# Eight products of low weights ahead of eight of high weights, in four chunks of a float32 encoder's up projections

## The chip, the cores and the metric

The kernel runs on one core of one Trainium2 chip. The metric is the device time of one execution in microseconds (us); the time of a kernel is the median of its runs. The profile is of one further execution.

## What is computed

The reference is a two-layer encoder on 256 tokens of width 2048, in float32. Each layer has a token mixer and then a gated channel mixer, each with a norm before and after and a residual add:

```python
def conv_glu(h, w_up, conv_w, conv_b, w_down):
    u = h @ w_up
    gate, val = u[..., :D_FF], u[..., D_FF:]
    gate = depthwise_conv3(gate, conv_w, conv_b)
    return (jax.nn.gelu(gate, approximate=False) * val) @ w_down
...
    for i in range(DEPTH):
        p = layers[i]
        h = rms_norm(x, p['mix_pre'])
        if i % 2 == 0:
            m = mixer_dilated_gqa(h, *p['mixer'], pos, row, col)
        else:
            m = mixer_mla(h, *p['mixer'], pos)
        x = x + rms_norm(m, p['mix_post'])
        h = rms_norm(x, p['ffn_pre'])
        x = x + rms_norm(conv_glu(h, *p['ffn']), p['ffn_post'])
```

The change concerns `h @ w_up` alone, with D_FF = 5632: half of its columns make the gate, half the value.

## The kernel before

**High and low halves.** TensorE multiplies in a rounded 32-bit format (F32R). To keep float32 accuracy, each operand is parted in two: a high half, which is the rounded number, and a low half, which is what the rounding left. A product of two numbers is then high x high + high x low + low x high.

**Weights.** All weights come as chunks of 128 x 1024 float32 (512 KB), in one fixed list. SyncE loads a chunk into one of four `raw` buffers (line 103). ScalarE casts it to the high half `whi` (line 117), and VectorE subtracts that from `raw` and writes the low half `wlo` (line 118). Both halves have three buffers each. `weights()` is called once per chunk: it sees that the chunks up to two ahead of the one it returns are split, and that the next ones are loading. The cast of the chunk three ahead has to wait until TensorE has read the high buffer that it will overwrite, and the subtraction in the same way for the low buffer.

**The up projection.** `ffn` loops over 11 groups of 512 gate columns and 512 value columns. For each group it calls `proj_t` twice: the gate projection (accumulators tagged `acc`) and then the value projection (tagged `at`). Here the weights are the stationary operand and the normed input is the moving one. The input tile of a block k has 512 columns: its high half for the 256 tokens, then its low half. So one product of high weights (line 186, 512 columns wide) gives high x high and high x low side by side in one accumulator, and one product of low weights (line 187, 256 wide) adds low x high to the first 256 columns; the two column halves are added later by `joined`. A `proj_t` has 8 chunks of weights, numbered 0 to 7, and four accumulators; a chunk holds two blocks k for each of the four accumulators, so it makes 8 high and 8 low products, high and low in turn. Each product brings its own load of 128 x 128 weights.

**What else runs.** While a value projection goes on, ScalarE and VectorE finish the gate of the same group (lines 247 to 248 and 911 to 917) and split the coming chunks. Between them the instructions of an engine stand in the order in which a scheduler put them; waits between engines are semaphores.

**Other products that the prediction speaks of.** `mm3` (lines 172 to 174) makes the three products of a block one after another. In `proj_pair` (layer 1) all of them are 256 wide, with weights as the stationary operand; in `proj_tok`, as the output projection of layer 0 uses it, all are 512 wide.

Of the kernel before, what the change touches and what calls it, by code (L numbers as in the profile page):

```python
# [16 lines left out]
P = 128  # L17
T = 256
D = 2048
KD = D // P  # L20
# [17 lines left out]
class Model:  # L38
# [134 lines left out]
        mm(ps, lh, rl, start=False, stop=False)  # L173
        mm(ps, ll, rh, start=False, stop=stop)  # L174

    def proj_t(self, nk, x, tag):

        mm = self.nc.tensor.matmul
        out = [self.psum(tag) for _ in range(4)]
        for c in range(nk // 2):  # L180
            hi, lo = self.weights()
            for i in range(4):
                for kk in range(2):
                    k = 2 * c + kk
                    s = slice(kk * 512 + i * P, kk * 512 + (i + 1) * P)
                    mm(out[i], hi[:, s], x(k), start=k == 0, stop=False)  # L186
                    mm(out[i][:, :T], lo[:, s], x(k)[:, :T], start=False, stop=k == nk - 1)  # L187
            self.tick()
        return out

# [703 lines left out]
    def ffn(self, layer, pre):  # L894
        nc, tc = self.nc, self.tc
        with tc.tile_pool(name=f"ffn{layer}", bufs=1) as sp:
            xs = self.xhl
            x = lambda k: xs[k // 4][:, k % 4].rearrange("p a t -> p (a t)")
            gh = [sp.tile([P, 4, T], F32R, name=f"gh{i}") for i in range(NFG)]
            gl = [sp.tile([P, 4, T], F32R, name=f"gl{i}") for i in range(NFG)]  # L900
            cw = lambda j, c: self.gain(f"l{layer}_conv_w", j * KF + c)
            norm = self.now(self.pre_norm(sp))
            for gi in range(NFG):
                pg = self.proj_t(KD, x, "acc")
                self.finish(norm)
                act = []
                for i in range(4):
                    c = 4 * gi + i
                    g = self.joined(sp, sp.tile([P, T], F32, tag="g", name="g", bufs=2), pg[i])
                    y = sp.tile([P, T], F32, tag="yf", name="yf", bufs=4)  # L910
                    nc.vector.tensor_tensor(out=g, in0=g, in1=self.rb, op=ALU.mult)
                    nc.scalar.activation(y, g, AF.Identity, scale=cw(1, c), bias=self.gain(f"l{layer}_conv_b", c))
                    nc.vector.scalar_tensor_tensor(out=y[:, 1:], in0=g[:, :T - 1], scalar=cw(0, c), in1=y[:, 1:],
                                                   op0=ALU.mult, op1=ALU.add)
                    nc.vector.scalar_tensor_tensor(out=y[:, :T - 1], in0=g[:, 1:], scalar=cw(2, c),
                                                   in1=y[:, :T - 1], op0=ALU.mult, op1=ALU.add)
                    nc.scalar.activation(y, y, AF.Gelu)
                    act.append(y)
                pv = self.proj_t(KD, x, "at")
                for i in range(4):  # L920
                    u = self.joined(sp, sp.tile([P, T], F32, tag="u", name="u", bufs=2), pv[i])
                    nc.vector.tensor_tensor(out=u, in0=u, in1=self.rb, op=ALU.mult)
                    nc.vector.tensor_tensor(out=u, in0=u, in1=act[i], op=ALU.mult)
                    self.parted(gh[gi][:, i, :], gl[gi][:, i, :], u)
            g = lambda k: (gh[k // 4][:, k % 4, :], gl[k // 4][:, k % 4, :])
            return self.out_proj(KF, g, 2 * layer + 1, pre, (sp, "m3", 1))
# [22 lines left out]
    def all_chunks(self):  # L949
        a = self.a  # L950
        groups = lambda w, gs: [w[g, c] for g in gs for c in range(w.shape[1])]
        out = groups(a["w_in0"], [8, 6, 7, 0, 2, 4, 1, 3, 5])
        out += [a["w_out0"][g, c] for g in range(4) for c in (4, 5, 6, 7, 0, 1, 2, 3)]
        ffn = lambda l: groups(a[f"w_up{l}"], [g for j in range(NFG) for g in (j, NFG + j)]) + \
            groups(a[f"w_down{l}"], range(4))
        out += ffn(0)
        out += groups(a["w_in1"], [0, 1]) + [a["w_kr"]]
        for p in range(8):
            out += groups(a["w_qr"], [p // 4]) if p % 4 == 0 else []
            out += [a["w_qn"][p], a["w_kn"][p]]  # L960
            out += groups(a["w_v"], [p // 2]) if p % 2 == 0 else []
        out += groups(a["w_out1"], range(4))
        out += ffn(1)
        return out
# [67 lines left out]
```

## Time and profile before

| | us |
|---|---|
| median of 3 runs | 2072.75 |
| lowest and highest of them | 2072.56, 2081.7 |
| the profiled execution | 2072.57 |
| its span, first to last instruction | 2070.8 |
| TensorE busy in the span | 2057.9 |
| VectorE busy | 1340.6 |
| ScalarE busy | 1084.6 |

Engines in the profile are PE (TensorE's products), PEld (its weight loads), DVE (VectorE), ACT (ScalarE), POOL and SP. A row of a group gives the line, engine, operation, the tiles written and read, shape and count; then the busy time in us and the mean of one in ns; then the idle time ahead of them and what ended it. A row of a timeline gives the start in us from the start of the span, the duration in us, engine, line, operation and count; a bracket gives the idle time before it and what released it. The granted clock of TensorE was 0.999 of full speed.

### The profile page before, as it was taken

How to read it: one execution, taken by the hardware profiler on the slowest of the kernel's cores; microseconds unless marked ns; L12 is line 12 of the kernel's file. 1: busy time of each engine (PE TensorE's matmuls, PEld its weight loads, DVE VectorE, ACT ScalarE, POOL GpSimd, SP SyncE). 2: the span in 40 equal slices, each digit the busy share in tenths (PEclk: the TensorE clock that was granted, in tenths of full speed). 3: DMA queues.
4: the chain of work that ended last, by engine and by line, in shares of the span. 5: the costliest groups of instructions: out<-in, count | busy, mean ns of one | idle time of the engine just before them, and what ended most of it. 6: DMA issues, size and time to landing. Idle time of an engine off the chain costs nothing.

```text
span 2070.8 us, 28951 instructions
## 1 busy us (share of the span) xinstructions
PE 2057.9 (99%) x10977; PEld 1764.1 (85%) x10977; DVE 1340.6 (65%) x2051; ACT 1084.6 (52%) x1695; POOL 0.2 (0%) x4
## 2 busy tenths in 40 slices
PE   9999999999999999999999999999999999999998
PEld 7888888888888888888888998888888888888886
DVE  6877757667667667444466875666766766754444
ACT  6655546555555555344455654555555555544443
POOL 0000000000000000000000000000000000000000
PEclk9999999999999999999999999999999999999999
DMA  8545565666666666666665445566666666666664
GB/s 315 176 153 163 164 200 174 186 193 190 188 192 191 187 192 190 196 198 199 198 186 170 125 129 177 177 188 190 185 195 191 188 191 190 185 200 198 198 194 154
DMA packets 108716, 385.96 MB, mean 186 GB/s; under 512 B 12064, under 2 KB 12576, under 8 KB 108576
## 3 DMA queue, kind: packets, MB, share of 16 engines
q1 hardware_dynamic: 108288, 383.83, 60.6%
q8 instruction: 86, 1.41, 0.3%
q14 instruction: 54, 0.44, 0.1%
q10 hardware_dynamic: 288, 0.28, 0.0%
HBM read 381.96 MB, written 2.10 MB: 185 GB/s over the span
## 4 chain that ended last, share of the span: by engine, by line
PE 98%; DVE 1%; ACT 0%; DMA 0%; issue 0%; DVEq 0%; SPq 0%
PE ps L186 31%; PE ps L172 16%; PE ps L174 16%; PE ps L173 16%; PE ps L187 16%; PE ps L463 1%; PE ps L242 1%; DVE x L383 1%; PE ps L405 0%; DMA raw<-in_w_in 0%; PE ps L790 0%; DVE wlo L118 0%; ACT junk L282 0%; PE ps L238 0%; DVE xhl L517 0%
## 5 line engine op out<-in xcount | busy, mean ns | idle before, releaser
L118 DVE TENSOR_TENSOR wlo<-raw,whi 128x1024 fp32r<-128x1024 f32 (+1 forms) x710 | 867.9, 1223 | 672.1 <-ACT whi L117 670.4
L117 ACT CAST whi<-raw 128x1024 fp32r<-128x1024 f32 (+1 forms) x710 | 745.9, 1052 | 786.5 <-PE ps L174 417.5
L186 PE MATMUL ps<-xhl,whi 128*128 128x512 f32 x2816 | 978.6, 394 | 1.0 <-DVE xhl L517 1.0
L187 PE MATMUL ps<-xhl,wlo 128*128 128x256 f32 x2816 | 779.2, 277 | 0.0
L186 PEld LDWEIGHTS ps<-xhl,whi 128*128 128x128 f32 x2816 | 527.6, 188 | 123.2 <-DVE xhl L517 1.9
L187 PEld LDWEIGHTS ps<-xhl,wlo 128*128 128x128 f32 x2816 | 528.7, 188 | 1.1 <-DVE wlo L118 0.5
L172 PE MATMUL ps<-whi,gh 128*128 128x512 f32 x704 | 273.9, 389 | 0.0
L174 PE MATMUL ps<-whi,gl 128*128 128x512 f32 x704 | 273.9, 389 | 0.0
L173 PE MATMUL ps<-wlo,gh 128*128 128x512 f32 x704 | 273.9, 389 | 0.0
L174 PEld LDWEIGHTS ps<-whi,gl 128*128 128x128 f32 x704 | 132.2, 188 | 27.7
L173 PEld LDWEIGHTS ps<-wlo,gh 128*128 128x128 f32 x704 | 132.2, 188 | 27.4
L172 PEld LDWEIGHTS ps<-whi,gh 128*128 128x128 f32 x704 | 132.2, 188 | 27.1
L172 PE MATMUL ps<-whi,xhl 128*128 128x512 f32 x352 | 138.8, 396 | 1.3 <-ACT whi L117 1.2
L173 PE MATMUL ps<-wlo,xhl 128*128 128x512 f32 x352 | 137.6, 391 | 0.0
L174 PE MATMUL ps<-whi,xhl 128*128 128x512 f32 x352 | 137.1, 391 | 0.0
L172 PE MATMUL ps<-whi,oh 128*128 128x512 f32 x256 | 100.0, 390 | 0.0
L173 PE MATMUL ps<-wlo,oh 128*128 128x512 f32 x256 | 99.7, 389 | 0.0
L174 PE MATMUL ps<-whi,ol 128*128 128x512 f32 x256 | 99.6, 389 | 0.0
L247 ACT COPY half<-ps 128x256 f32<-128x256 f32 x176 | 65.0, 369 | 45.6 <-PE ps L186 36.0
L172 PEld LDWEIGHTS ps<-whi,xhl 128*128 128x128 f32 x352 | 66.0, 188 | 15.1 <-ACT whi L117 1.5
L174 PEld LDWEIGHTS ps<-whi,xhl 128*128 128x128 f32 x352 | 66.0, 188 | 13.9
L173 PEld LDWEIGHTS ps<-wlo,xhl 128*128 128x128 f32 x352 | 66.3, 188 | 13.4 <-DVE wlo L118 0.9
(186 smaller groups left out, 1584.9 us busy)
## 6 DMA issues: line engine op xcount, KB each, us to landing
raw<-in_w_up SPq DMA_DIRECT2D x352, 512.0 KB, 4.1
raw<-in_w_down SPq DMA_DIRECT2D x176, 512.0 KB, 4.2
raw<-in_w_in SPq DMA_DIRECT2D x88, 512.0 KB, 3.8
raw<-in_w_out SPq DMA_DIRECT2D x64, 512.0 KB, 3.9
gb<-in_post SPq DMA_DIRECT2D x16, 256.0 KB, 3.9
raw<-in_w_qn SPq DMA_DIRECT2D x8, 512.0 KB, 3.6
raw<-in_w_kn SPq DMA_DIRECT2D x8, 512.0 KB, 3.6
raw<-in_w_v SPq DMA_DIRECT2D x8, 512.0 KB, 3.6
```

The lines of the kernel that those rows point to most:

```text
L117: self.nc.scalar.copy(hi[:, s], raw[:, s])
L118: self.nc.vector.tensor_tensor(out=lo[:, s], in0=raw[:, s], in1=hi[:, s].bitcast(F32), op=ALU.subtract)
L172: mm(ps, lh, rh, start=start, stop=False)
L173: mm(ps, lh, rl, start=False, stop=False)
L174: mm(ps, ll, rh, start=False, stop=stop)
L186: mm(out[i], hi[:, s], x(k), start=k == 0, stop=False)
L187: mm(out[i][:, :T], lo[:, s], x(k)[:, :T], start=False, stop=k == nk - 1)
L242: self.tc.keep_in_program_order(self.nc.tensor.transpose(out, x, self.ident))
L247: self.nc.scalar.copy(b, ps[:, T:])
L383: return nc.vector.scalar_tensor_tensor(out=x, in0=m[c][:, t, s], scalar=r[t], in1=x, op0=ALU.mult, op1=ALU.add)
L463: nc.tensor.matmul(ps[:, i, :], l, r, start=n == 0, stop=n == len(pairs) - 1))
```

## The change

In `proj_t` a new argument `apart` names one chunk in which all eight low products come first and then all eight high ones, each in the same order of accumulators and blocks as before. In all other chunks high and low alternate as they did. `ffn` passes 4, the fifth of eight chunks, for the value projection of the first two groups, so four chunks of the program are concerned: two in each layer.

```diff
-    def proj_t(self, nk, x, tag):
+    def proj_t(self, nk, x, tag, apart=None):
...
             hi, lo = self.weights()
-            for i in range(4):
-                for kk in range(2):
-                    k = 2 * c + kk
-                    s = slice(kk * 512 + i * P, kk * 512 + (i + 1) * P)
-                    mm(out[i], hi[:, s], x(k), start=k == 0, stop=False)
-                    mm(out[i][:, :T], lo[:, s], x(k)[:, :T], start=False, stop=k == nk - 1)
+            blocks = [(i, 2 * c + kk, slice(kk * 512 + i * P, kk * 512 + (i + 1) * P))
+                      for i in range(4) for kk in range(2)]
+            high = lambda i, k, s: mm(out[i], hi[:, s], x(k), start=k == 0, stop=False)
+            low = lambda i, k, s: mm(out[i][:, :T], lo[:, s], x(k)[:, :T], start=False, stop=k == nk - 1)
+            for products in ((low,), (high,)) if c == apart else ((high, low),):
+                for b in blocks:
+                    for product in products:
+                        product(*b)
             self.tick()
...
-                pv = self.proj_t(KD, x, "at")
+                pv = self.proj_t(KD, x, "at", 4 if gi < 2 else None)
```

On TensorE, at the fifth chunk of layer 0's first value projection, this stands before. The four `ps` are the accumulators, `xhl2` the input, `whi_3507` and `wlo_3508` the halves of this chunk's weights; `wlo_3486` belongs to the chunk before.

```order
L187 MATMUL ps_3458<-xhl1_3171,wlo_3486 128x256
L186 MATMUL ps_3455<-xhl2_3244,whi_3507 128x512
L187 MATMUL ps_3455<-xhl2_3244,wlo_3508 128x256
L186 MATMUL ps_3455<-xhl2_3244,whi_3507 128x512
L187 MATMUL ps_3455<-xhl2_3244,wlo_3508 128x256
L186 MATMUL ps_3456<-xhl2_3244,whi_3507 128x512
L187 MATMUL ps_3456<-xhl2_3244,wlo_3508 128x256
L186 MATMUL ps_3456<-xhl2_3244,whi_3507 128x512
L187 MATMUL ps_3456<-xhl2_3244,wlo_3508 128x256
```

The other two accumulators go on in the same way. In the changed kernel the same place reads as follows (lines 187 and 188 are there what 186 and 187 are before, and `whi_3529` belongs to the next chunk):

```order
L188 MATMUL ps_3458<-xhl1_3171,wlo_3486 128x256
L188 MATMUL ps_3455<-xhl2_3244,wlo_3508 128x256 x2
L188 MATMUL ps_3456<-xhl2_3244,wlo_3508 128x256 x2
L188 MATMUL ps_3457<-xhl2_3244,wlo_3508 128x256 x2
L188 MATMUL ps_3458<-xhl2_3244,wlo_3508 128x256 x2
L187 MATMUL ps_3455<-xhl2_3244,whi_3507 128x512 x2
L187 MATMUL ps_3456<-xhl2_3244,whi_3507 128x512 x2
L187 MATMUL ps_3457<-xhl2_3244,whi_3507 128x512 x2
L187 MATMUL ps_3458<-xhl2_3244,whi_3507 128x512 x2
L187 MATMUL ps_3455<-xhl2_3244,whi_3529 128x512
```

The eight low products have moved ahead of the eight high ones; the three other chunks read alike, and nothing else on TensorE has moved. The instructions of VectorE, ScalarE and SyncE stand in the same order as before. Only a wait differs: on VectorE, the subtractions around chunk 7's (`wlo_3574`) with the engines and queues that each waits for, before:

```order
L118 TENSOR_TENSOR wlo_3508<-raw_3392,whi_3507 128x1024 [waits DMAHW4_49,PE_49,Activation_49]
L118 TENSOR_TENSOR wlo_3530<-raw_3467,whi_3529 128x1024 [waits DMAHW5_49,PE_49,Activation_49]
L118 TENSOR_TENSOR wlo_3552<-raw_3489,whi_3551 128x1024 [waits DMAHW6_49,PE_49,Activation_49]
L118 TENSOR_TENSOR wlo_3574<-raw_3511,whi_3573 128x1024 [waits DMAHW7_49,PE_49,Activation_49]
L118 TENSOR_TENSOR wlo_3596<-raw_3533,whi_3595 128x1024 [waits DMAHW0_49,PE_49,Activation_49]
```

and in the changed kernel:

```order
L118 TENSOR_TENSOR wlo_3508<-raw_3392,whi_3507 128x1024 [waits DMAHW4_49,PE_49,Activation_49]
L118 TENSOR_TENSOR wlo_3530<-raw_3467,whi_3529 128x1024 [waits DMAHW5_49,PE_49,Activation_49]
L118 TENSOR_TENSOR wlo_3552<-raw_3489,whi_3551 128x1024 [waits DMAHW6_49,PE_49,Activation_49]
L118 TENSOR_TENSOR wlo_3574<-raw_3511,whi_3573 128x1024 [waits DMAHW7_49,Activation_49]
L118 TENSOR_TENSOR wlo_3596<-raw_3533,whi_3595 128x1024 [waits DMAHW0_49,PE_49,Activation_49]
```

The subtraction of chunk 7 reuses the low buffer of chunk 4, and no longer waits for TensorE itself: the cast that it waits for has waited for a later product of that chunk.

## The prediction

> **What bounds the kernel now.** I read the page first, for what fills the span and for the chain that ended last; then the list of waits of TensorE's weight loads, since what the change turns round is the order in which TensorE asks for its two kinds of weights; then the timeline of TensorE, VectorE and ScalarE around the four chunks that change. The page's rows:
>
> ```profile
> span 2070.8 us, 28951 instructions
> PE 2057.9 (99%) x10977; PEld 1764.1 (85%) x10977; DVE 1340.6 (65%) x2051; ACT 1084.6 (52%) x1695; POOL 0.2 (0%) x4
> PE 98%; DVE 1%; ACT 0%; DMA 0%; issue 0%; DVEq 0%; SPq 0%
> L186 PE MATMUL ps<-xhl,whi 128*128 128x512 f32 x2816 | 978.6, 394 | 1.0 <-DVE xhl L517 1.0
> L187 PE MATMUL ps<-xhl,wlo 128*128 128x256 f32 x2816 | 779.2, 277 | 0.0
> L187 PEld LDWEIGHTS ps<-xhl,wlo 128*128 128x128 f32 x2816 | 528.7, 188 | 1.1 <-DVE wlo L118 0.5
> ```
>
> TensorE is busy for 99% of the span and makes up 98% of the chain that ended last. Nothing else sets the end, so the change is worth what it does to TensorE's stream of products, plus any idle time that it puts into that stream. The two lines that it reorders, 186 (a product of high weights, 512 columns wide) and 187 (of low weights, 256 wide), are the products of the up projections; they had practically no idle time ahead of them. Next, who kept the weight loads of line 187 waiting, over the whole program:
>
> ```profile
> engine line waited for: us in total, times, longest us
> PEld ps L187 <- DVE wlo L118: 0.5, 2, 0.3
> ```
>
> Twice in 2816 loads a low product found its low weights not yet written, and 0.5 us was lost. That is the dependence that the change draws forward, and the profile says that it almost never binds. Then one of the four changed chunks, the fifth of layer 0's first value projection, on TensorE's timeline (start, duration, engine, line):
>
> ```profile
> 368.23 0.39 PE L186 MATMUL ps<-xhl,whi 128*128 128x512 f32 x1
> 368.46 0.27 PE L187 MATMUL ps<-xhl,wlo 128*128 128x256 f32 x1
> 368.57 0.40 PE L186 MATMUL ps<-xhl,whi 128*128 128x512 f32 x1
> ...
> 370.65 0.40 PE L186 MATMUL ps<-xhl,whi 128*128 128x512 f32 x1
> 370.88 0.28 PE L187 MATMUL ps<-xhl,wlo 128*128 128x256 f32 x1
> 371.00 0.39 PE L186 MATMUL ps<-xhl,whi 128*128 128x512 f32 x1
> ```
>
> What to see here is the spacing of starts, not the durations. A low product follows its high one after 0.23 us, the next high one after 0.11, and the chunk of sixteen takes 371.00 - 368.23 = 2.77 us. The printed durations add up to 8 x (0.394 + 0.277) = 5.4 us, twice that; the page says that matmuls are pipelined and that their ends are modelled. So I cost the change by distances between starts. The four changed chunks together are 4 x 2.77 = 11.1 us of the 2070.8.
>
> **Part 1, the same products in another order.** Nothing is added or removed: eight high and eight low products before, and eight of each after. What changes is which product follows which. A chunk was eight times high-low and low-high; it becomes seven times low-low, once low-high, seven times high-high and once high to the next chunk's high. The trace has long runs of both new neighbours elsewhere. The pair projection of layer 1 issues 24 products of 256 columns one after another, and the output projection of layer 0 issues 33 of 512 columns; of each run the first and the last row:
>
> ```profile
> 1128.89 0.28 PE L172 MATMUL ps<-ckv,whi 128*128 128x256 f32 x1
> 1131.63 0.28 PE L174 MATMUL ps<-ckv,wlo 128*128 128x256 f32 x1
> 319.78 0.39 PE L172 MATMUL ps<-whi,oh 128*128 128x512 f32 x1
> 327.04 0.40 PE L174 MATMUL ps<-whi,ol 128*128 128x512 f32 x1
> ```
>
> The narrow run has 23 steps in 2.74 us, 0.119 us a step; the wide run has 32 steps in 7.26 us, 0.227 a step. Every product in them brings its own weight load, as here, and consecutive ones add into the same accumulator, as here. A changed chunk is then 8 x 0.119 + 8 x 0.227 = 0.953 + 1.815 = 2.77 us, against 2.77 now. The difference is under the 0.01 us in which the timeline is printed: a narrow product costs 0.01 more behind a narrow one than a wide product costs behind it, and a wide one saves as much by not standing ahead of a narrow one. I take 0.00 us a chunk.
>
> The bounds come from further rows. The best that the narrow products could do is the 0.11 us seen in the chunk above between a low start and the next; 8 x 0.11 + 1.815 = 2.70, a gain of 0.07 a chunk and 0.3 us over four. The worst is that a run of low products is paced by its weight loads, each with the 0.188 us of the page's row: 8 x (0.188 - 0.119) = 0.55 us a chunk, 2.2 us in all. Were it paced by the whole modelled product of 0.277, that would be 8 x (0.277 - 0.119) = 1.26 a chunk, 5.1 us in all. The nearest row by far is the narrow run, with the same shape, the same kind of weights and the same accumulation, and it decides.
>
> The Trainium skill, page "TensorE: Matmul & The Clock Gate", section "LDWEIGHTS (loading the stationary operand)", gives a weight load as its columns divided by 1.2 in ns: an estimate of 107 ns for 128 columns, not the recorded 188. By the page a load just fits under a narrow product and the sum stays 0.00; by the recorded load it would be +2.2 us. The narrow run's 0.119 us a step agrees with the page.
>
> The Trainium skill, page "Perfetto Trace Analysis", section "Tensor Engine Instruction (MATMUL, LD_WEIGHTS)", adds that the end of a matmul is computed from its size, not observed. By that the 277 ns is no price and the 5.1 us falls away; the 2.77 us chunk against 5.4 us of durations bears it out.
>
> **Part 2, the low weights are wanted first.** The first product of the chunk waited for the cast of the high half (ScalarE, line 117) and the second, 0.23 us later, for the subtraction that makes the low half (VectorE, line 118). Now the first one waits for VectorE. Behind that wait stand all the later products in TensorE's queue, so a late subtraction would cost its full lateness. The four subtractions that belong to the four chunks, and the starts of the three other chunks:
>
> ```profile
> 365.30 1.22 DVE L118 TENSOR_TENSOR wlo<-raw,whi 128x1024 fp32r<-128x1024 f32 x1
> 409.68 1.22 DVE L118 TENSOR_TENSOR wlo<-raw,whi 128x1024 fp32r<-128x1024 f32 x1
> 1365.48 1.22 DVE L118 TENSOR_TENSOR wlo<-raw,whi 128x1024 fp32r<-128x1024 f32 x1
> 1409.86 1.23 DVE L118 TENSOR_TENSOR wlo<-raw,whi 128x1024 fp32r<-128x1024 f32 x1
> 412.60 0.39 PE L186 MATMUL ps<-xhl,whi 128*128 128x512 f32 x1
> 1368.41 0.39 PE L186 MATMUL ps<-xhl,whi 128*128 128x512 f32 x1
> 1412.79 0.39 PE L186 MATMUL ps<-xhl,whi 128*128 128x512 f32 x1
> ```
>
> The low halves are ready at 366.52, 410.90, 1366.70 and 1411.09, and the chunks start at 368.23, 412.60, 1368.41 and 1412.79. That is 1.71, 1.70, 1.71 and 1.70 us of cover, after the 0.23 us by which the demand moves forward has been taken off. What hides the edit is that weights are split two chunks ahead of their use; if that cover were gone, the cost would be what the subtraction is late by. Cost 0.
>
> **Part 3, the buffers come free at other times.** Each half has three buffers, so the cast for chunk 7 waits for the last high product of chunk 4. On ScalarE's timeline that cast, then the subtraction behind it on VectorE's, then the start of chunk 7 on TensorE's:
>
> ```profile
> 371.08 1.05 ACT L117 CAST whi<-raw 128x1024 fp32r<-128x1024 f32 x1 [1.72 <-PE ps L186]
> 372.17 1.23 DVE L118 TENSOR_TENSOR wlo<-raw,whi 128x1024 fp32r<-128x1024 f32 x1 [1.55 <-ACT whi L117]
> 376.55 0.39 PE L186 MATMUL ps<-xhl,whi 128*128 128x512 f32 x1
> ```
>
> The last high product starts at 370.65 now, and becomes the last product of the chunk: 371.00 - 0.23 = 370.77. So the cast starts 0.12 us later, at about 371.20, and its subtraction ends at about 373.52 instead of 373.40. Chunk 7 starts at 376.55, so 3.0 us of cover are left. The next cast waits for chunk 5 and doesn't feel it. The low half of chunk 4 comes free about 1.8 us earlier (its last reader starts near 369.07, not 370.88), and the subtraction of chunk 7 loses its wait for TensorE; but it was released by the cast (the row says so), so it gains nothing. The queues of the loads, of ScalarE and of the output are not reordered. Cost 0.
>
> The sum is 0.00 + 0 + 0, four times. The profiled execution took 2072.57 us, of which 2070.8 are its span and 1.8 lie around it; the median of the three runs is 2072.75, 0.2 above. I forecast 2072.6 us.
>
> **The rivals.** *A run of narrow products is paced by its weight loads* (slower). Place: the first half of each changed chunk. It decides as soon as one load in a row of them takes TensorE longer than the 0.119 us step. Price 2.2 us with the recorded 0.188, giving 2074.8, and 5.1 with the modelled 0.277, giving 2077.7. For it speaks the recorded load, longer than the step; against it stand 23 steps at 0.119, each with such a load. I give it 0.05.
>
> *The early demand for the low half is met late* (slower). It decides once VectorE ends the subtraction over 1.7 us later than in the rows above; a whole further subtraction put in ahead (1.22) would not do it. Two of them ahead would be 0.7 us late, 3 us over four chunks, giving 2075.6. VectorE's order is unchanged, so I give it 0.02.
>
> *The alternation itself costs something* (faster). If the narrow products in a row took 0.11, the gain is 0.3 us, giving 2072.3; earlier free low buffers could add at most the 0.5 us of waits on line 187, giving 2071.8. I give it 0.05, mostly for the first half of it. That the change does nothing at all is excluded for the order on TensorE, which does change in these four places.
>
> **How the numbers follow.** My forecast of no change gets 0.83, the three rivals 0.12, and 0.05 is left for something that these rows don't show. A measurement of this kernel can tell about 0.5% from no change, 10.4 us, and that is nearly as long as the four changed chunks together: to be slower by so much they would have to take almost twice their time, and to be faster by so much they would have to vanish. Every case above therefore lies within 0.5%. The 0.05 is divided as 0.02 faster and 0.03 slower, the larger part on the slow side because one of the three runs shown lies at 2081.7, 9 us above the other two. So faster 0.02, same 0.95, slower 0.03. The range runs from 2070.5, which is the lowest case less about 1 us for another run, to 2077.7, the dearest bound.
>
> **What would show it right or wrong.** In the profile of the changed kernel each of the four chunks should show eight low starts about 0.12 apart, then eight high ones about 0.23 apart, 2.77 us from the first to the next chunk's first. Part 1 is wrong if the low starts stand 0.15 or more apart, or if high products behind high ones stand nearer than 0.22. Part 2 is wrong if the weight loads of the low products wait for line 118 more often than twice. Part 3 is wrong if chunk 7's cast moves by more than 0.2 us, or if a product of chunk 7 waits. The forecast as a whole is wrong if the span moves by more than 5 us, and then its cause would have to lie outside these chunks.

## The result, and the profile after

| | us |
|---|---|
| changed kernel, median of 5 runs | 2089.95 (2089.70 to 2090.27) |
| kernel before, median of 5 runs, the three shown above among them | 2072.65 (2072.56 to 2081.70) |
| ratio | 1.0075, 95% interval 1.0054 to 1.0095 |
| span of the profiled execution | 2087.9, before 2070.8 |

The change costs 17.3 us, 0.75%. The range ended at 2077.7: the forecast of no change was wrong. The page of the changed kernel:

```profile
span 2087.9 us, 28951 instructions
PE 2076.0 (99%) x10977; PEld 1772.8 (85%) x10977; DVE 1340.3 (64%) x2051; ACT 1081.4 (52%) x1695; POOL 0.2 (0%) x4
PE 98%; DVE 1%; ACT 0%; DMA 0%; issue 0%; DVEq 0%; SPq 0%
L187 PE MATMUL ps<-xhl,whi 128*128 128x512 f32 x2816 | 992.3, 399 | 1.0 <-DVE xhl L522 1.0
L188 PE MATMUL ps<-xhl,wlo 128*128 128x256 f32 x2816 | 784.1, 281 | 0.0
```

TensorE waits no more than it did. It is busy for 99% again, with the same number of products, and its busy time has grown by 18 us. Only the two lines of the up projection became dearer (lines 187 and 188 are 186 and 187 of before); the large groups of `mm3`, 389 to 396 ns each before, are where they were. So the time lies in products that run at a lower pace, not in a gap. Where they lie shows in the answer for the line of the high products, asked for each layer apart: behind the count stand the shortest, median and longest duration in ns, then the starts of the first and of the last product in us. In the kernel before:

```profile
L186 PE MATMUL ps<-xhl,whi x1408: 387/395/501, 331.3 to 822.7; 128*128 128x512 f32 x176
L186 PE MATMUL ps<-xhl,whi x1408: 390/395/504, 1331.6 to 1822.9; 128*128 128x512 f32 x176
```

In the changed kernel:

```profile
L187 PE MATMUL ps<-xhl,whi x1408: 387/398/500, 331.1 to 831.1; 128*128 128x512 f32 x176
L187 PE MATMUL ps<-xhl,whi x1408: 389/398/505, 1340.0 to 1840.0; 128*128 128x512 f32 x176
```

The up projection took 491.4 and 491.3 us and takes 500.0 and 500.0 now: 8.6 + 8.7 = 17.3 us, the whole result. Next the changed chunk itself on TensorE's timeline. Neighbours of one line are merged, so the nine low products begin with the last one of chunk 3, and the nine high ones end with the first one of chunk 5:

```profile
367.88 1.23 PE L188 MATMUL ps<-xhl,wlo 128*128 128x256 f32 x9
368.94 2.23 PE L187 MATMUL ps<-xhl,whi 128*128 128x512 f32 x9
371.01 0.28 PE L188 MATMUL ps<-xhl,wlo 128*128 128x256 f32 x1
```

From the last low product of chunk 3 to the first high one stand nine steps in 1.06 us, 0.118 each; from there to the next low one nine in 2.07, 0.230 each. That is close to the 0.119 and 0.227 of the prediction, and a chunk that costs nearly what it did. But 130 us later, in chunks whose order was not touched, the stream looks otherwise than in the kernel before, which shows this:

```profile
499.96 0.39 PE L186 MATMUL ps<-xhl,whi 128*128 128x512 f32 x1
500.19 0.27 PE L187 MATMUL ps<-xhl,wlo 128*128 128x256 f32 x1
500.31 0.40 PE L186 MATMUL ps<-xhl,whi 128*128 128x512 f32 x1
500.54 0.28 PE L187 MATMUL ps<-xhl,wlo 128*128 128x256 f32 x1
500.65 0.39 PE L186 MATMUL ps<-xhl,whi 128*128 128x512 f32 x1
```

The changed kernel at the same time:

```profile
500.05 0.40 PE L187 MATMUL ps<-xhl,whi 128*128 128x512 f32 x1
500.28 0.28 PE L188 MATMUL ps<-xhl,wlo 128*128 128x256 f32 x1
500.40 0.40 PE L187 MATMUL ps<-xhl,whi 128*128 128x512 f32 x1
500.64 0.28 PE L188 MATMUL ps<-xhl,wlo 128*128 128x256 f32 x1
500.76 0.40 PE L187 MATMUL ps<-xhl,whi 128*128 128x512 f32 x1
501.00 0.28 PE L188 MATMUL ps<-xhl,wlo 128*128 128x256 f32 x1
501.11 0.40 PE L187 MATMUL ps<-xhl,whi 128*128 128x512 f32 x1
```

Before, the pattern repeats every two pairs (0.39, 0.27, 0.40, 0.28) in 0.69 us. After, it repeats every three pairs in 1.06 us, with steps of 0.24 between a high and a low product, which the other pattern doesn't have. From the third group to the last chunk, 143 chunks, a chunk takes 2.773 us in the one and 2.827 us in the other. In a layer 162 chunks of the old order follow the first changed one: 162 x 0.0533 = 8.6 us. I call the two a rhythm of two pairs and a rhythm of three pairs.

**Theory:** the alternating stream has more than one stable rhythm; the changed chunk breaks the running one, the stream falls into the three-pair rhythm, and it stays there until the projection ends. **Rivals:** each changed chunk costs 17.3 / 4 = 4.3 us of its own; or ScalarE, VectorE and the loads have come into another phase to TensorE and disturb it; or the new program as such is slower (where its code or buffers lie).

### The profile page after: what moved, and what is told of

It is laid out like the page before. It is cut to its first block, busy times and chain, and to the rows that moved or that the text cites. A ratio compares the mean times of both kernels' runs of the same rounds, so it can differ in the third digit from the quotient of the medians.

```text
span 2087.9 us, 28951 instructions
## 1 busy us (share of the span) xinstructions
PE 2076.0 (99%) x10977; PEld 1772.8 (85%) x10977; DVE 1340.3 (64%) x2051; ACT 1081.4 (52%) x1695; POOL 0.2 (0%) x4
## 4 chain that ended last, share of the span: by engine, by line
PE 98%; DVE 1%; ACT 0%; DMA 0%; issue 0%; DVEq 0%; SPq 0%
PE ps L187 32%; PE ps L188 16%; PE ps L172 16%; PE ps L173 16%; PE ps L174 16%; PE ps L468 1%; PE ps L247 1%; DVE x L388 1%; PE ps L410 0%; DMA raw<-in_w_in 0%; PE ps L795 0%; DVE wlo L118 0%; ACT junk L287 0%; PE ps L243 0%; DVE xhl L522 0%
## 5 line engine op out<-in xcount | busy, mean ns | idle before, releaser
L187 PE MATMUL ps<-xhl,whi 128*128 128x512 f32 x2816 | 992.3, 399 | 1.0 <-DVE xhl L522 1.0
```

The costliest lines, as they stand in the source:

```text
L187: high = lambda i, k, s: mm(out[i], hi[:, s], x(k), start=k == 0, stop=False)
```

## The experiments

All edits are against the changed kernel; the last experiment has none. Over the experiments the runs of the kernel before fell into three groups, near 2072.6, 2081.5 and, three times, 2090.5; what these are is shown by the last experiment, and medians are to be compared with 2072.6.

**Changed chunks only in the last group.**

```diff
-                pv = self.proj_t(KD, x, "at", 4 if gi < 2 else None)
+                pv = self.proj_t(KD, x, "at", 4 if gi == NFG - 1 else None)
```

> The changed chunk is moved from the first two groups to the eleventh, last one, of each layer: two changed chunks in all. Rhythm theory (the alternating stream of products has two steady rhythms, 0.347 and 0.353 us a pair; a changed chunk throws it into the slow one, which lasts to the end of the layer's up projection): only 3 chunks of 8 pairs follow in each layer, 2 x 24 x 0.0063 = 0.3 us, so 2073.0. If each changed chunk instead costs 17.3 / 4 = 4.3 us wherever it stands: 2081.3. If the mere presence of such chunks slows the whole program (placement of code or buffers): about 2090.

Measured: median 2073.15 us, ratio 1.0012 (0.9989 to 1.0035). The same reordering, placed at the end of the stream, is nearly free: the six shorter runs lie between 2072.62 and 2073.34. So a changed chunk has no price of 4.3 us of its own. Of the other four runs three lay near 2081.6 and one at 2090.5, as runs of the kernel before do.

**Changed chunks only in the first group.**

```diff
+                pv = self.proj_t(KD, x, "at", 4 if gi == 0 else None)
```

> The changed chunk is kept in the first group of each layer and dropped in the second: two changed chunks. Rhythm theory: the first one has thrown the stream into the slow rhythm and nothing brings it back, 163 chunks of 8 pairs in each of two layers at 0.0063 us more, 16.4 us and the transients, so 2089 to 2090, as with four. A price for each changed chunk: 2072.7 + 8.6 = 2081.3.

Measured: 2089.98 us, ratio 1.0069 (1.0043 to 1.0096). Two changed chunks cost as much as four. The price lies in what follows.

**A break behind the changed chunks.**

```diff
+                if gi == 2:
+                    self.warm(1)
                 pg = self.proj_t(KD, x, "acc")
```

> The changed kernel with one small product of zeros (bfloat16, 256 wide) issued ahead of the third group of each layer: a break in the stream after both changed chunks. Rhythm theory: the break is an occasion to fall into either rhythm. If it falls into the fast one, the slow stretch is from chunk 4 of the first value projection to the end of the second group, 20 chunks in each layer: 2 x 20 x 0.05 = 2 us, so 2075; if into the slow one, 2090. If side engines or the placement of code slow the stream, one small product changes nothing: 2090. So 2075 would speak for a rhythm alone; 2090 would leave it open.

Measured: 2074.81 us, all ten runs between 2074.49 and 2075.10, ratio 0.9992 (0.9976 to 1.0009). The line of the high products, by layer:

```profile
L187 PE MATMUL ps<-xhl,whi x1408: 387/395/505, 331.2 to 823.6; 128*128 128x512 f32 x176
L187 PE MATMUL ps<-xhl,whi x1408: 389/395/504, 1332.6 to 1825.0; 128*128 128x512 f32 x176
```

492.4 us in each layer instead of 500.0: one product of zeros in each layer, ahead of the third group, takes 15.1 of the 17.3 us back. The changed chunks are all still there. The rival of the new program as such falls with this run, and that of a price for each changed chunk once more.

**Without the side traffic.** In groups 4 to 8 every chunk uses one and the same pair of weight halves, and the list of weights to load leaves those groups out, so the kernel computes something else.

```diff
+            if keep is None or c == 0 and not self.kept:
+                self.kept = self.weights()
+            hi, lo = self.kept
...
+                keep = True if 4 <= gi < 9 else None
```

> The changed kernel, but in groups 4 to 8 of each layer (counted from 0) every chunk uses one and the same pair of weight halves: no weights are loaded, cast or subtracted there, and 80 chunks of each layer have only the gate and value work on ScalarE and VectorE beside the products. The output is therefore another. Rhythm theory: the slow rhythm is TensorE's own, and these chunks still take 2.83 us. Contention theory (from the changed chunk on, ScalarE, VectorE or the loads stand in another phase to TensorE and take its memory accesses): with that traffic gone the chunks take 2.77 us or less.

Measured: 2089.98 us in its one run. A stretch of 50 us in the frozen groups (length, busy time and instructions of PE, PEld, DVE, ACT and POOL, granted clock, DMA share, GB/s):

```profile
600.00:650.00 50.00, 50.00 (x284) 43.35 (x284) 13.10 (x34) 8.90 (x22) 0.00 (x0) 1.00 0.00 1
```

The same stretch of the changed kernel:

```profile
600.00:650.00 50.00, 50.00 (x285) 43.39 (x284) 32.65 (x50) 26.33 (x40) 0.00 (x0) 1.00 0.65 188
```

And of the kernel before:

```profile
600.00:650.00 50.00, 50.00 (x290) 43.68 (x289) 35.97 (x62) 27.58 (x43) 0.00 (x0) 1.00 0.64 189
```

With no loads and well under half of the work on VectorE and ScalarE, TensorE gets through 284 products, against 285 in the changed kernel and 290 before. In 45 of the 80 frozen chunks of layer 0 neither VectorE nor ScalarE ran any instruction, and those took 2.82 to 2.83 us each as well. So contention doesn't hold the slower rhythm, and the granted clock is the same in all three.

**High products first.**

```diff
-            for products in ((low,), (high,)) if c == apart else ((high, low),):
+            for products in ((high,), (low,)) if c == apart else ((high, low),):
```

> In the same four chunks the eight high products precede the eight low ones. After the chunk, the alternation then begins with a high product behind a low one, as it always does in the kernel before, and not behind a high one. If it is the entry behind a high product that throws the stream into the slow rhythm: fast afterwards, about 2072.7. If any chunk with its products grouped does it: about 2090. If each changed chunk had a price of its own of 4.3 us: about 2090 too, but with the time in the four chunks.

Measured: 2090.14 us, ratio 1.0071 (1.0045 to 1.0097), with chunks of 2.83 us behind the first changed one, as in the changed kernel. My guess that the entry behind a high product counts is refuted; either grouping leads into the three-pair rhythm.

**One exchanged pair.**

```diff
-            for products in ((low,), (high,)) if c == apart else ((high, low),):
+            for products in ((high, low),):
...
+                    for product in reversed(products) if c == apart and b is blocks[0] else products:
```

> In the same four chunks only the first two products change places (low, high, then high, low and so on as before): one low product behind a low one and one high product behind a high one. If the entry behind a high product is what counts: the slow rhythm, about 2090. If it takes a whole run of eight: fast, about 2072.7 in most runs.

Measured: 2088.45 us, ratio 1.0056 (1.0033 to 1.0079). But the two exchanges did not act alike. Behind the one in the first group the chunks stayed at 2.77 us, in a third rhythm that repeats with every pair (steps of 0.230 and 0.117); behind the one in the second group they took 2.83 us. The same edit has two outcomes, so what decides is what it meets.

**One small product ahead of the chunk, in the old order.**

```diff
+            if c == apart:
+                self.warm(1)
+            for products in ((high, low),):
```

> The order of the kernel before, all chunks alternating; ahead of chunk 4 of the first two value projections of each layer stands one small product of zeros (bfloat16, 256 wide). Rhythm theory: as in the run with a later break, the stream falls into the fast rhythm behind it, in every run: 2072.5 to 2073.5 and no run near 2081.6, where some runs of the kernel before lie (one layer slow from its first chunks on, 176 x 0.05 = 9 us). If a break can go either way, runs near 2090 or 2081.6 appear.

Measured: 2090.23 us, ratio 1.0072 (1.0046 to 1.0098). That was expected the other way: here the break led into the three-pair rhythm, by the time in all four runs. No product is reordered in this kernel, and still it costs the 17 us.

**The small product one pair later.** The old order again, with the product of zeros behind the first pair.

```diff
+                    if c == apart and b is blocks[1]:
+                        self.warm(1)
```

> The small product of zeros stands one pair later than in the run that it is to be compared with: behind the first pair of chunk 4 of the first two value projections, not ahead of it. If the rhythm that follows depends on where in the running rhythm the break falls, this can come out fast (about 2072.7) where the other was slow (2090.2). If any such break leads into the slow rhythm: 2090 again.

Measured: 2088.86 us, ratio 1.0054 (1.0031 to 1.0078). The total hides that the first break did come out the other way. TensorE's timeline around it, in the run with the break ahead of the chunk:

```profile
368.16 0.40 PE L187 MATMUL ps<-xhl,whi 128*128 128x512 f32 x1
368.39 0.28 PE L188 MATMUL ps<-xhl,wlo 128*128 128x256 f32 x1
368.51 0.29 PE L156 MATMUL ps<-zeros 128*128 128x256 bf16 x1
...
369.69 0.40 PE L187 MATMUL ps<-xhl,whi 128*128 128x512 f32 x1
369.93 0.28 PE L188 MATMUL ps<-xhl,wlo 128*128 128x256 f32 x1
```

And in this one:

```profile
368.16 0.39 PE L187 MATMUL ps<-xhl,whi 128*128 128x512 f32 x1
368.39 0.27 PE L188 MATMUL ps<-xhl,wlo 128*128 128x256 f32 x1
368.50 0.28 PE L156 MATMUL ps<-zeros 128*128 128x256 bf16 x1
...
369.67 0.40 PE L187 MATMUL ps<-xhl,whi 128*128 128x512 f32 x1
369.90 0.28 PE L188 MATMUL ps<-xhl,wlo 128*128 128x256 f32 x1
```

Behind the pair with 0.40 and 0.28 the break led into the three-pair rhythm (step 0.24 at 369.69); behind the pair with 0.39 and 0.27 the stream went on in two pairs. Only the second group's break, which fell behind a pair of 0.40 and 0.28 again, made this run long. The two breaks stand at the same place of their chunks, so it is the place in the rhythm that differs, not the one in the program.

**The break alone.** The kernel before, with the small product ahead of the third group.

```diff
+                if gi == 2:
+                    self.warm(1)
                 pg = self.proj_t(KD, x, "acc")
...
-                pv = self.proj_t(KD, x, "at", 4 if gi < 2 else None)
+                pv = self.proj_t(KD, x, "at")
```

> The kernel before with one small product of zeros ahead of the third group of each layer, and no grouped chunks. In the run that had both, this break led from the slow rhythm into the fast one in ten runs of ten. Here it meets a stream in the fast rhythm in most runs. If it leads into the fast one from there too: 2072.7, and the runs near 2081.6 shrink to 2073 to 2075.5. If it throws the fast stream into the slow rhythm: 2 x 144 chunks x 0.05 = 14.5 us more, 2087.

Measured: 2088.25 us, ratio 1.0049 (1.0028 to 1.0070): 15.65 us above 2072.6, where 144 chunks in each of two layers at 0.0533 make 15.4. Three of its twelve runs lay near 2081.8; none of these was profiled. The break that healed the changed kernel spoils the one before. In the profile it too fell behind a pair of 0.40 and 0.28, in both layers.

**Exchange in the first group alone.** The exchanged pair as above, with `4 if gi == 0 else None`.

> One exchanged pair in chunk 4 of the first value projection of each layer and none in the second. In the run with both, the first exchange left the stream in a rhythm of one pair, 0.3467 us, and the second threw it into the slow one. Rhythm theory: the stream stays in the rhythm of one pair to the end of the layer, 164 chunks of 2.773 in place of 2.776 us, about 1 us less than the fast runs of the kernel before: 2071.5 to 2072.7. If an exchange costs time wherever it is, 2080.

Measured: median 2072.68 us and all twelve runs between 2072.45 and 2072.94; ratio to all runs of the kernel before 0.9976 (0.9959 to 0.9993). The gain of about 1 us that I expected for the one-pair rhythm isn't there: a chunk takes 2.773 us in it, as in that of two pairs. Layer 0 of the profiled execution happens to have begun in the three-pair rhythm; the exchange at 368 us takes it out:

```profile
365.66 0.40 PE L187 MATMUL ps<-xhl,whi 128*128 128x512 f32 x1
...
366.72 0.40 PE L187 MATMUL ps<-xhl,whi 128*128 128x512 f32 x1
...
368.01 0.40 PE L188 MATMUL ps<-xhl,wlo 128*128 128x256 f32 x2
368.25 0.64 PE L187 MATMUL ps<-xhl,whi 128*128 128x512 f32 x2
...
369.19 0.39 PE L187 MATMUL ps<-xhl,whi 128*128 128x512 f32 x1
369.54 0.39 PE L187 MATMUL ps<-xhl,whi 128*128 128x512 f32 x1
```

Three pairs in 1.06 us ahead of it (365.66 to 366.72), one pair in 0.35 behind it. Of the 35 runs of the kernel before on the same chip, 20 lay between 2072.30 and 2072.84, 12 between 2081.37 and 2081.63 and 3 between 2090.27 and 2091.56; this version had none of the longer ones. It is the version of this study that I would keep.

**Exchange behind the grouped chunk.**

```diff
+                pv = self.proj_t(KD, x, "at", 4 if gi < 2 else None, gi == 1)
...
+                    for product in reversed(products) if one and c == apart and b is blocks[0] else products:
```

> The changed chunk in the first group of each layer, and in chunk 4 of the second value projection only the first two products exchanged. Rhythm theory: the grouped chunk leads into the slow rhythm, and the exchanged pair leads out of it into the rhythm of one pair, as it did in the profile in which layer 0 had begun slow. Slow are then 16 chunks in each layer, 2 x 16 x 0.05 = 1.6 us and the transients: 2074 to 2074.5 in every run. If the exchange leads out of the slow rhythm only from some places in it: 2090, or 2082.

Measured: 2090.15 us, ratio 1.0057 (1.0035 to 1.0079). The exchange did not lead out here. It met the three-pair rhythm at another place: behind a low product that followed its high one by 0.24, not by 0.23. So neither break nor exchange is a sure remedy.

**Orders without alternation.** In all chunks the eight high products first, and in another run two high and two low of each accumulator.

```diff
+            for products in ((high,), (low,)):
```
```diff
+            for i in range(0, 8, 2):
+                for product in (high, low):
+                    for b in blocks[i:i + 2]:
+                        product(*b)
```

> In all 352 chunks of the up projections the eight high products precede the eight low ones, so there is no alternation left to fall into a slow rhythm. By the steady steps of long runs (0.227 and 0.119) a chunk takes 2.77 us, some 0.01 less than alternating, about 2070 to 2073; if each change from low to high disturbs the next steps as in the changed kernel's four chunks (2.79 us in place of 2.77): 352 x 0.015 = 5 us more, about 2078. Under either no run should stand 9 or 17 us above the others.

> In all chunks of the up projections the two high products of an accumulator come first and then its two low ones (high, high, low, low). There is no stream of alternating products left that could fall into the slow rhythm of the kernel before. By the steps between starts (high-high 0.227, high-low 0.231, low-low 0.119, low-high 0.117) four products take 0.694 us, as two alternating pairs do in the fast rhythm: 2072 to 2073 and no run 9 us above. If this order has slow rhythms of its own, some or all runs stand at 2080 or more.

Measured: 2079.41 us (2079.25 to 2079.54), ratio 1.0022 (1.0009 to 1.0035), and 2077.87 us (2077.65 to 2077.99), ratio 1.0004 (0.9987 to 1.0021), the ratios against all runs of the kernel before. Neither has longer runs, but a chunk takes 2.793 and 2.787 us, so both lose to 2.773 and win against 2.827. The steps of long runs do not add up to the cost of a mixed order.

**The kernel before, profiled three times more.**

> The kernel before itself, to catch one of its runs at 2081.5 in a profile. Rhythm theory: about two in three runs take 2072.6 and show 2.77 us a chunk in both layers; a run at 2081.5 shows 2.83 us in one layer from its first value projection on and 2.77 in the other. If those runs have another cause, all chunks of both layers, or other stages, are longer.

> The same kernel as in the run ahead, for a second chance of a run at 2081.5, with the same expectation.

> The same kernel as in the two runs ahead, for a third chance of a run at 2081.5, with the same expectation.

They took 2090.41, 2081.56 and 2072.61 us, one of each group. The high products by layer, in the run of 2081.56:

```profile
L186 PE MATMUL ps<-xhl,whi x1408: 390/398/501, 331.3 to 831.5; 128*128 128x512 f32 x176
L186 PE MATMUL ps<-xhl,whi x1408: 387/395/505, 1340.4 to 1831.8; 128*128 128x512 f32 x176
```

500 us in layer 0 and 491 in layer 1; in the run of 2090.41 it is 500 in both. The kernel before has both rhythms. Which one a layer gets comes out of the disturbed first chunks, in which the products wait for the norm and share TensorE with transposes, and the traces show the place where it is settled. The last other products in the stream are four short ones for the norm's factors (line 309), between the first gate projection and the first value projection. The last pair ahead of them in layer 0, in the profile of before, which goes on in two pairs:

```profile
356.32 0.40 PE L186 MATMUL ps<-xhl,whi 128*128 128x512 f32 x1
356.57 0.28 PE L187 MATMUL ps<-xhl,wlo 128*128 128x256 f32 x1
```

And in the run of 2081.56, whose layer 0 goes on in three:

```profile
356.23 0.39 PE L186 MATMUL ps<-xhl,whi 128*128 128x512 f32 x1
356.46 0.28 PE L187 MATMUL ps<-xhl,wlo 128*128 128x256 f32 x1
```

The first is the long step of the three-pair rhythm, 0.241 before the starts are rounded. In the second all pairs ahead have 0.39 and 0.28 at steps of 0.23, the one-pair rhythm. The 16 profiles of kernels whose first chunks alternate as before have 32 such places. In 20 the four products met the three-pair rhythm behind its long step, and in 7 the two-pair rhythm behind a pair of 0.39 and 0.27; all 27 layers went on in two pairs. In 5 they met the one-pair rhythm, and all 5 went on in three.

Of the 83 timed runs 51 lay near 2072.6, 29 near 2081.5 and 3 near 2090.5. With one such layer in a run near 2081.5 and two in one near 2090.5, the stream runs in three pairs in (29 + 2 x 3) / 166 = 0.21 of the layers. In the five runs of the changed kernel both layers are there, by their times.

## Why the prediction was wrong

**The bound** was right: TensorE's stream sets the end, before and after.

**Part 1 failed.** The step that failed is the sum "eight narrow steps, eight wide steps, 2.77 against 2.77, 0.00 us a chunk" as the whole price of the order. Inside the chunk it holds nearly: 2.79 us. It put what the chunk does to the products behind it at nothing, and gave no reason. The 0.23 and 0.11 us of the alternating stream are not properties of the two products but of a rhythm. The chunks that I read in the trace of before showed one kind; the step of 0.24 stood in it too, ahead of 356.7 us. All the products behind the chunk belonged in the sum: 162 chunks a layer x 0.0533 us x 2 = 17.3 us. The runs with the change in the last group alone (2073.15) and in the first alone (2089.98) show it: same edit, different length of stream behind it.

**Part 2 held.** The low weights kept TensorE waiting twice for 0.5 us in all, as before:

```profile
PEld ps L188 <- DVE wlo L118: 0.5, 2, 0.3
```

**Part 3 held.** The cast of chunk 7, its subtraction and the start of that chunk in the changed kernel:

```profile
370.98 1.05 ACT L117 CAST whi<-raw 128x1024 fp32r<-128x1024 f32 x1 [1.86 <-PE ps L187]
372.06 1.23 DVE L118 TENSOR_TENSOR wlo<-raw,whi 128x1024 fp32r<-128x1024 f32 x1 [1.68 <-ACT whi L117]
376.42 0.40 PE L187 MATMUL ps<-xhl,whi 128*128 128x512 f32 x1
```

The cast starts 2.98 us after the chunk's first product (at 367.88 + 0.12 = 368.00, the second of the nine merged low ones), against 2.85 before: 0.13 later, for 0.12 foretold. The cover left is 376.42 - 373.29 = 3.1 us.

**The rivals.** A run of low products paced by its loads: no, 0.118 a step. Low weights late: no. Alternation that costs something: no; every other order that was run in all chunks was dearer than the two-pair rhythm. The result lay in the 0.05 that I had left for what the rows didn't show, of which 0.03 were for slower. In the rows above, the signs that I had named for the single parts held: they looked only at the four chunks and their buffers; the last one, that a move of over 5 us would have its cause outside these chunks, pointed the right way, but named no mechanism.

**The sign that I read past.** One of the three runs shown stood at 2081.7, 9 us above the others. I took it for scatter; it moved 0.01 of the chances to the slow side. It was half the result: a layer in the three-pair rhythm costs 8.6 us. A kernel whose runs fall into separate groups has states, and a change can pick between them.

**What stays open.** Why the stream has these rhythms, and which of TensorE's parts holds the memory of them, no run here shows. The place of a break within the rhythm went with the outcome in all twelve breaks of the four profiles that have them, but only the break put one pair later was a test of that, and no run varied the place further. What makes the first chunks of a layer reach the four products of line 309 in one rhythm or another is open too.

## What to carry to other kernels

On an engine that is busy for 99%, cost a change of order by the stream behind it as well: compare the step between starts far from the edit, not only at it. Where the runs of a kernel fall into groups, find out what a group is before a difference of that size is called an effect of an edit. A single exchanged pair early in a long stream can settle it in the better rhythm, but the place must be found by trial and checked over many runs.

## What the runs showed of the hardware

A stream of alternating 512- and 256-column products on TensorE ran in three stable rhythms at the same granted clock of 0.999: 0.3467 us a pair in repeats of one or two pairs, and 0.3533 in repeats of three (a chunk's eight pairs in 2.773 and 2.827 us). It kept its rhythm for over 150 chunks, past waits of other engines and with the loads gone. A chunk of the other orders took 2.787 and 2.793 us. In order of size these four means lie two, one and five times 0.00667 us apart, within 0.001 us.

In the profiles with a small product and no grouped chunk, a break that met the two-pair rhythm behind the pair that the profile prints with 0.40 and 0.28 led into the three-pair rhythm (6 of 6), and one behind the pair with 0.39 and 0.27 kept that of two (2 of 2). The next high product starts 0.118 us behind the low one of the first kind of pair, and 0.113 behind that of the second. In the three-pair rhythm a break behind the long step of 0.24 led out (2 of 2, in the run with the break behind the changed chunks), and one a pair later did not (2 of 2, in the run with the small product ahead of the chunk).
